# Attention's product with v for two steps at a time, in every second step

## The chip, the cores and the metric

The kernel runs on one core of one Trainium2 chip. The metric is the device time of one execution in microseconds (us); the figure for a kernel is the median over its runs. Single numbers about engines come from one profiled execution.

## The reference, cut to what matters

One encoder layer, for a prompt of 256 positions and a sample of 2048 positions, with the same weights. Positions form a grid of rows of 64. All of it is in float32.

```python
def encoder_layer(x, ...):
    h = rms_norm(x, g_pre)
    q, k, v, z_a, u_f, z_f = split(h @ w_in)
    y_a = neighbourhood_attention(q, k, v, rpb)     # 8 heads of 64; a window of 8 rows x 16 columns
    y_f = fourier_mix(u_f, w_fourier, b_fourier)
    mixed = concat([rms_norm(y_a, g_na) * silu(z_a), rms_norm(y_f, g_f) * silu(z_f)])
    return x + rms_norm(mixed @ w_out, g_post)

# neighbourhood_attention, for 16 query columns of a row against a slab of 8 rows x 32 columns
logits = q_blk @ k_slab.T * scale + bias            # outside the window: -1e30
p = softmax(logits)
out = p @ v_slab
```

## The kernel before, in words

The kernel first makes the projections (until 549 us of the profiled execution), then the Fourier branch (until about 613 us), then a loop over attention steps (613 to 865 us), and at the end the output product of the attention half. The change is in the loop over steps.

**Groups.** Attention is cut into 36 groups `G[0..35]`: four pairs of heads (`pr`), and for each pair nine groups (`i`): the prompt, and four bands of sample rows in two halves of columns each (`hc`). A group has 256 queries in two blocks `b` of 128, each with its own slab of keys, and two heads `h`.

**A step.** Step `k` (2 to 36) works on two neighbouring groups, `g = G[k]` and `f = G[k-1]`. The order in which TensorE gets its work is written by hand, and so are those of the other engines and of the DMA queue on SyncE: every engine does its instructions strictly in the order of the code. On TensorE a step is:

1. `scores(g)`: 12 products of q and k into four PSUM tiles `s`. Each is split in a high and a low part: `qh` with `kh`, `qh` with `kl`, and, last, `ql` with `kh`. They use 64 of the 128 rows of the array, one half for each head.
2. `transp(f, 0)`: the exponentials of the previous group's first block are transposed into the PSUM tiles `ptb`; ScalarE (head 0) and VectorE (head 1) copy them to a tile `pt`.
3. Six products of the Fourier half's output, `po` (`f_mm`), 128 x 512.
4. `transp(f, 1)`, and its copies.
5. Six more products of `po`.
6. `pv(f)`: the product of `pt` with v, into a PSUM tile `p` of tag `c`, of which there is one. They use 64 of the 128 columns of the array, one half for each head.

**The other engines in a step.** VectorE adds the bias and takes the maximum (`bias_max`, L1203, four times), ScalarE takes the exponential with its sum (`exps`, L1208, four times), VectorE inverts the sums and GpSimd scales (`soft`, L1215). `split_q(G[k+1])` makes the next group's `qh` on ScalarE (L1163) and `ql` on GpSimd (L1164); in ScalarE's order it stands behind the four exponentials and the copies of both transposes. `f_evac` takes `po` out of PSUM, on VectorE for even `k` (L1464), on ScalarE for odd `k` (L1461), where every second one is stored to `oD`. After `pv`, VectorE multiplies the result by the gate `za` into `y` (L1516) and ScalarE squares it (L1518 for the first pair of heads; L1522 for the others, where GpSimd adds the squares up, L1523).

**Buffers.** `pt` is a tag with two buffers of 4 KB, one for each block of a group. `v` and `za` have three buffers each. `gt` hands out tiles from a ring of 13 tiles of 4 KB; during the loop eight of them hold `wo1`, the weights of `po`, and the others take the tiles `ofs`, which `f_evac` fills.

Of the kernel before, what the change touches and what calls it, by code (L numbers as in the profile page):

```python
# [10 lines left out]
F32 = mybir.dt.float32  # L11
# [25 lines left out]
PB = 2  # L37
# [131 lines left out]
def build(tc, A, O):  # L169
# [44 lines left out]
    ps = es.enter_context(tc.tile_pool(name="ps", bufs=3, space=PSUM))  # L214
# [16 lines left out]
    def gt(shape, dtype, name):  # L231
        return gp.tile(shape, dtype, tag="g", name=name)
# [527 lines left out]
    for b in range(16):  # L760
# [13 lines left out]
        if 2 <= b < 8:  # L774
            x, y = divmod(b, 2)
# [7 lines left out]
        p = mmt(512)[:, :TP]  # L783
# [3 lines left out]
        o = st.tile([128, 256], F32, tag="f", name="f", bufs=3)  # L787
# [51 lines left out]
    for i in range(16):  # L839
        sg, pr = divmod(i, 8)  # L840
# [14 lines left out]
        o = [st.tile([128, 1024], F32, tag="f", name="f", bufs=3) for x in range(2)]  # L855
# [32 lines left out]
        for j in range(7):  # L888
# [29 lines left out]
            if sg == 0:  # L918
                x, y = divmod(7 * (pr - 1) + j, 14)
# [17 lines left out]
            for f, d in ((u_load, 0), (u_split, 4), (u_stage1, 6)):  # L937
                x = 7 * pr + j - 7 - d
# [11 lines left out]
            p = mmt(512)  # L950
# [166 lines left out]
    def group(pr, i):  # L1117
        if i == 0:
            return dict(pr=pr, R=None, ts=slice(0, TP), k0=0, nr=4, t=[(24 * b, 40) for b in range(2)])
        R, hc = divmod(i - 1, 2)  # L1120
        t0 = TP + 512 * R + 256 * hc
        return dict(pr=pr, R=R, hc=hc, ts=slice(t0, t0 + 256), k0=4 + K0[R], nr=NR[R],
                    t=[(KC0[2 * hc + b], KW[2 * hc + b]) for b in range(2)])
# [91 lines left out]
            nc.gpsimd.tensor_scalar(w, w, m[:, 4 + h:5 + h], 1.0, ALU.mult, ALU.mult)  # L1215

    G = [group(pr, i) for pr in range(4) for i in range(9)]

    sc = load_k(0)
    KK = {0: load_k(0)}  # L1220
# [5 lines left out]
    mask_p(0)  # L1226
    for g in G[:2]:
        prep(g)
# [3 lines left out]
    for n in range(2):  # L1232
        for c in range(4):
            nc.sync.dma_start(wo1[n][c].bitcast(F32),
                              woD[1, :, c, :, n * 512:n * 512 + 512].rearrange("x p d -> p x d"))
    prep(G[2])
    prep(G[3])
    for g in G[:2]:
        split_q(g)
# [3 lines left out]
    y0 = sqy.tile([128, 2, 4, 128], F32, name="y0")  # L1243
    for t, (g, x) in enumerate(zip(G, (0, 640))):
        g["w"] = []
# [69 lines left out]
    for e in range(4):  # L1315
# [26 lines left out]
        py = y_mm(e, 2)  # L1342
        scores(G[0])
        first_soft(G[0], lambda: y_out(e, 2, *py))
# [24 lines left out]
    pt = ExitStack()  # L1369
    jp = pt.enter_context(tc.tile_pool(name="jp", bufs=2))  # L1370
# [109 lines left out]
    def transp(g, b):  # L1480
        ch = g["ch"][b]
        n, z = len(ch) * 128, ch[0][1]
        o = jp.tile([128, 2, 512], F32, tag="pt", name="pt", bufs=PB)
        for h in range(2):
            for j, (c0, nk, v) in enumerate(ch):
                nc.tensor.transpose(ptb[h][:nk, j * 128:j * 128 + 128], g["w"][b][:, h, c0:c0 + nk], ident)  # L1486
            if h == 0:
                nc.scalar.copy(o[:z, h, :n], ptb[h][:z, :n])
            else:
                V.tensor_copy(o[:z, h, :n], ptb[h][:z, :n])  # L1490
        g["pt"] = g.get("pt", []) + [o]

    yt = {}

    def pv(g):
        pr, R = g["pr"], g["R"]
        p = ps.tile([128, 2, 128], F32, tag="c", name="pv", bufs=1)
        for b, ch in enumerate(g["ch"]):
            for j, (c0, nk, v) in enumerate(ch):
                for h in range(2):  # L1500
                    hs = slice(64 * h, 64 * h + 64)
                    nc.tensor.matmul(p[hs, b], g["v"][:nk, v, hs], g["pt"][b][:nk, h, j * 128:j * 128 + 128],  # L1502
                                     start=j == 0, stop=j == len(ch) - 1)
        if R is None:
            ts, hc, c = slice(0, TP), 0, 32
            za = g["za"].rearrange("p (b r c) -> p b r c", b=2, c=32)
            view = lambda a: a.rearrange("p (r b c) -> p b r c", b=2, c=32)
        else:
            ts, hc, c = slice(TP + 512 * R, TP + 512 * R + 512), g["hc"], 16
            za = g["za"].rearrange("p (r b c) -> p b r c", b=2, c=16)  # L1510
            view = lambda a: a.rearrange("p (r x b c) -> p x b r c", x=2, b=2, c=16)[:, hc]
        p4 = p.rearrange("p b (r c) -> p b r c", c=c)
        if hc == 0:
            yt[0] = jp.tile([128, 512], F32, tag="y", name="y", bufs=YB)
        y = yt[0][:, :ts.stop - ts.start]
        V.tensor_tensor(out=view(y), in0=p4, in1=za, op=ALU.mult)  # L1516
        if pr == 0:
            nc.scalar.activation(view(ysq[:, ts]), p4, AF.Square)  # L1518
        else:
            sq = jp.tile([128, 256], F32, tag="sqa", name="sqa", bufs=2)  # L1520
            s4 = sq.rearrange("p (b r c) -> p b r c", b=2, c=c)
            nc.scalar.activation(s4, p4, AF.Square)  # L1522
            nc.gpsimd.tensor_tensor(out=view(ysq[:, ts]), in0=view(ysq[:, ts]), in1=s4, op=ALU.add)  # L1523
        if R is None or hc:
            nc.sync.dma_start(yD[0, pr, :, ts], y)
# [19 lines left out]
    f_mm(1)  # L1545
    ys_split(ftiles[1])
    f_evac(1)
    pv(G[0])
    ys_load(ftiles[2])
    prep_v(G[2])  # L1550
    prep(G[4])
    for k in range(2, len(G) + 1):
        pr, i = divmod(k, 9)
        g, f = G[k] if k < len(G) else None, G[k - 1] if k else None
        if pr < 3:
            if i == 3:
                KK[pr + 1] = load_k(pr + 1)
                for x in range(2):
                    fetch_k(KK[pr + 1], pr + 1, x)
            if i == 7:  # L1560
                load_t(pr + 1, 0)
        if 0 < pr < 4 and i == 0:
            load_t(pr, 1)
        if pr < 4 and i == 3:
            load_t(pr, 2)
        if k == 9:
            nc.sync.dma_start(gpb, pbc(A["gpost"]))
        if k == 23:
            wp = pt.enter_context(tc.tile_pool(name="wp", bufs=1, side="right"))
            WO.extend(wp.tile([128, 4, D], F32R, name="w0%d" % x) for x in range(2))  # L1570
        if 24 <= k < 32:
            y = k - 24
            nc.sync.dma_start(WO[y % 2][:, y // 2].bitcast(F32), woD[0, y % 2, y // 2])
        x = k // 2 + 1
        if g:
            scores(g)
            if 2 < k < 34 and k % 2 == 0:
                ys_mul(ftiles[x])
                if x + 1 < 18:
                    ys_load(ftiles[x + 1])  # L1580
            bias_max(g, 0, 0)
            exps(g, 0, 0)
            bias_max(g, 0, 1)
            bias_max(g, 1, 0)
        if f:
            transp(f, 0)
        if g:
            exps(g, 0, 1)
            bias_max(g, 1, 1)
            exps(g, 1, 0)  # L1590
            f_mm(k, range(6))
            soft(g, 0)
            exps(g, 1, 1)
            if k in NT:
                f_norm(NT[k])
            if k in (32, 34):
                a_norm(atiles[:6] if k == 32 else atiles[6:10])
        else:
            a_mm(atiles[0], 0, range(6))
            a_norm(atiles[10:14])  # L1600
        if f:
            transp(f, 1)
        if g:
            if k + 1 < len(G):
                split_q(G[k + 1])
            soft(g, 1)
            if k == 2:
                ys_mul(ftiles[x])
                ys_load(ftiles[x + 1])
        run_later()  # L1610
        for v, x0, x1 in YSQ.get(k, []):
            nc.scalar.activation(v[:, x0:x1], v[:, x0:x1], AF.Square)
            V.tensor_tensor(out=sqs[:, x0:x1], in0=sqs[:, x0:x1], in1=v[:, x0:x1], op=ALU.add)
        if g:
            f_mm(k, range(6, 12))
        else:
            a_mm(atiles[0], 0, range(6, 12))
        if pr < 3 and i == 8:
            mask_p(pr + 1)
        if k % 2 and x < 18:  # L1620
            ys_split(ftiles[x])
        if pr < 3 and i in (5, 6, 7, 8):
            split_k(KK[pr + 1], i - 5)
        if k == 34:
            ys_split(atiles[0])
        if g:
            f_evac(k)
        if f:
            pv(f)
        if k == 12:  # L1630
            pq_.close()
        if k + 1 < len(G):
            prep_v(G[k + 1])
        if k + 3 < len(G):
            prep(G[k + 3])
        if k == 28:
            xk = [kp.tile([128, T], F32, tag=x, name="xk") for x in ("kh", "kl")]
        if 32 <= k < 36:
            x, d = k - 32, atiles[k - 32]
            d["xt"] = xk[x // 2][:, x % 2 * D:x % 2 * D + D]  # L1640
            nc.sync.dma_start(d["xt"], A["xn"][d["t"] * 128:d["t"] * 128 + 128, :])
        if k == 32:
            ys_load(atiles[0])
        if k in (34, 35):
            ys_load(atiles[k - 33])
            of_load(atiles[k - 34])
        if k == 36:
            ys_split(atiles[1])
# [113 lines left out]
```

## Time and profile before

| | |
|---|---|
| median of 3 runs | 973.16 us (972.75 to 975.66) |
| the profiled execution | 971.13 us, its span 969.3 us |
| TensorE busy | 960.3 us (99%) |
| VectorE, ScalarE, GpSimd busy | 709.3, 496.7, 430.2 us (73%, 51%, 44%) |
| granted TensorE clock | 0.997 |
| HBM | 184.37 MB read, 101.72 MB written |

PE is TensorE's product and PEld its weight load, DVE is VectorE, ACT is ScalarE, POOL is GpSimd, SP is SyncE, which issues the DMAs. The span runs from the first to the last instruction; what lies between it and the time of the execution, 1.8 us, is outside the program's instructions. A row of the timeline gives the start, the duration, the engine, the line, the operation with the tiles written and read, and how many instructions are merged in it; in square brackets stands how long the engine sat idle before, and who ended that. A product's duration includes the time in which the next one already runs, so the pace of products is read from the difference of their starts. One product of `pv` stands in the trace as two records.

### The profile page before, as it was taken

The page shows a single profiled execution, that of the slowest core. Times are in us where ns is not written, and L with a number is a line of the kernel's source. Part 1 is how long each engine was busy: PE and PEld are TensorE (multiplying, and loading weights), DVE is VectorE, ACT ScalarE, POOL GpSimd, SP SyncE. Part 2 cuts the span into 40 slices and gives each one's busy share as a digit, 9 for nine tenths or more (in the row PEclk, how much of TensorE's full clock was granted, in tenths as well). Part 3 has the DMA queues.
Part 4 walks back from the last instruction along what each step waited for, and adds up shares of the span by engine and source line. Part 5 has one row for each costly group of instructions (what it writes and reads, how often), then busy time and mean ns, then how long its engine had stood idle before and what let it go on. Part 6 is the DMA issues. An engine that isn't in the chain of part 4 may idle for free.

```text
span 969.3 us, 17001 instructions
## 1 busy us (share of the span) xinstructions
PE 960.3 (99%) x5761; PEld 805.3 (83%) x5761; DVE 709.3 (73%) x1301; ACT 496.7 (51%) x1068; POOL 430.2 (44%) x400
## 2 busy tenths in 40 slices
PE   9999999999999999999999999999999999999997
PEld 7889988888888888888888879888888888888886
DVE  6758987778986867796776446776665656659997
ACT  5836675433325533333344255677666776654443
POOL 3100003464752202766655033567677686524544
PEclk9999999999999999999999999999999999999998
DMA  9899696556849996599888897697886998979993
GB/s 327 316 378 342 239 366 241 192 203 240 324 156 379 351 409 240 208 376 342 302 304 333 303 328 298 212 297 261 260 238 222 289 328 270 286 243 343 333 345 126
DMA packets 146450, 279.89 MB, mean 289 GB/s; under 512 B 13162, under 2 KB 84284, under 8 KB 142972
## 3 DMA queue, kind: packets, MB, share of 16 engines
q1 hardware_dynamic: 145932, 278.41, 82.4%
q8 instruction: 46, 0.75, 0.3%
q10 hardware_dynamic: 432, 0.39, 0.1%
q14 instruction: 40, 0.33, 0.1%
HBM read 184.37 MB, written 101.72 MB: 295 GB/s over the span
## 4 chain that ended last, share of the span: by engine, by line
PE 97%; DVE 1%; POOL 1%; issue 0%; DMA 0%; ACT 0%; DVEq 0%; SPq 0%; POOLq 0%; ACTq 0%
PE po L1432 20%; PE mm L165 18%; PE mm L166 18%; PE mm L164 18%; PE pv L1502 5%; PE ptb L1486 5%; PE s L1181 4%; PE pab L1024 2%; PE py L164 1%; PE py L166 1%; PE py L165 1%; DMA gpre<-gpre 0%; PE ppq L1062 0%; PE pz L166 0%; PE pz L165 0%
## 5 line engine op out<-in xcount | busy, mean ns | idle before, releaser
L164 PE MATMUL mm<-xh,wa 128*128 128x512 f32 x448 | 174.4, 389 | 0.0
L165 PE MATMUL mm<-xl,wa 128*128 128x512 f32 x448 | 174.3, 389 | 0.0
L166 PE MATMUL mm<-xh,wa 128*128 128x512 f32 x448 | 174.3, 389 | 0.0
L536 POOL TENSOR_TENSOR ws<-wr 128x512 f32<-128x512 f32 x16 | 23.7, 1483 | 226.9 <-DMA wr<-wz 212.9
L1215 POOL TENSOR_SCALAR w<-w,m 128x480 f32<-128x480 f32 (+6 forms) x136 | 86.3, 647 | 44.5 <-DVE m L1212 39.3
L165 PEld LDWEIGHTS mm<-xl,wa 128*128 128x128 f32 x448 | 84.1, 188 | 17.5
L164 PEld LDWEIGHTS mm<-xh,wa 128*128 128x128 f32 x448 | 84.1, 188 | 17.5
L166 PEld LDWEIGHTS mm<-xh,wa 128*128 128x128 f32 x448 | 84.1, 188 | 17.4
L1432 PE MATMUL po<-wo,yh 128*128 128x512 f32 x272 | 90.5, 413 | 0.0
L551 DVE TENSOR_TENSOR wa<-wr,wa 128x512 fp32r<-128x512 f32 x60 | 68.6, 1152 | 27.9 <-ACT wa L550 27.7
L1208 ACT ACTIVATE w<-w,m 128x480 f32<-128x480 f32 (+6 forms) x136 | 79.3, 586 | 15.2 <-DVE m L1203 15.2
L1432 PE MATMUL po<-w,yh 128*128 128x512 f32 x280 | 86.7, 391 | 0.0
L1203 DVE CUSTOM_DVE_ANT_1 w<-s,tb 128x360 f32<-128x360 f32 (+5 forms) x124 | 62.5, 541 | 8.1 <-PE s L1181 7.3
L589 POOL TENSOR_TENSOR mt<-mt,rmask 128x880 f32<-128x880 f32 (+2 forms) x24 | 51.1, 2141 | 33.9 <-DVE mt L585 27.4
L165 PE MATMUL mm<-vl,xh 128*128 128x512 f32 x168 | 65.5, 390 | 0.2 <-DVE vl L482 0.2
L164 PE MATMUL mm<-vh,xh 128*128 128x512 f32 x168 | 65.4, 389 | 0.0
L166 PE MATMUL mm<-vh,xl 128*128 128x512 f32 x168 | 65.4, 389 | 0.0
L877 DVE TENSOR_TENSOR f<-u,mm 128x512 f32<-128x512 f32 x64 | 43.5, 680 | 28.1 <-PE mm L166 23.5
L1432 PEld LDWEIGHTS po<-w,yh 128*128 128x128 f32 x280 | 52.3, 188 | 10.8 <-issue 0.2
L1486 PE MATMUL ptb<-ident,w 128*120 128x128 f32 (+5 forms) x428 | 59.6, 277 | 0.1
L550 ACT CAST wa<-wr 128x512 fp32r<-128x512 f32 x60 | 36.4, 617 | 45.1 <-PE mm L166 18.8
L1490 DVE COPY pt<-ptb 120x384 f32<-120x384 f32 (+6 forms) x72 | 41.0, 570 | 24.5 <-PE ptb L1486 24.0
(253 smaller groups left out, 2402.9 us busy)
## 6 DMA issues: line engine op xcount, KB each, us to landing
wr<-wz SPq DMA_DIRECT2D x48, 512.0 KB
vl<-sD SPq DMA_DIRECT2D x20, 512.0 KB
xm<-xm SPq DMA_DIRECT2D x9, 1024.0 KB
oD<-ofs SPq DMA_DIRECT2D x18, 512.0 KB
of<-oD SPq DMA_DIRECT2D x18, 512.0 KB
yr<-yD SPq DMA_DIRECT2D x34, 256.0 KB
zD<-f SPq DMA_DIRECT2D x16, 512.0 KB
woD<-wo SPq DMA_DIRECT2D x16, 512.0 KB
```

Source lines behind the costliest of these rows:

```text
L164: nc.tensor.matmul(out, lh, rh, start=first, stop=False)
L165: nc.tensor.matmul(out, lh, rl, start=False, stop=False)
L166: nc.tensor.matmul(out, ll, rh, start=False, stop=last)
L551: nc.vector.tensor_tensor(out=o[:, 1], in0=src, in1=o[:, 0].bitcast(F32), op=ALU.subtract)
L589: nc.gpsimd.tensor_tensor(out=o, in0=i, in1=rmask[:, m0:m0 + n].unsqueeze(2).to_broadcast([128, n, 80]), op=ALU.add)
L877: nc.vector.tensor_tensor(out=dst(f, b), in0=src(uu[u]), in1=src(p), op=op)
L1203: nc.vector.tensor_tensor_reduce(out=rows(g["w"][b][:, h, :n], w), in0=rows(g["s"][2 * b + h][:, :n], w), in1=tv, scale=1.0, scalar=3.0e38 ...
L1208: nc.scalar.activation(w, w, AF.Exp, bias=m[:, h:h + 1], scale=-1.0, accum_out=m[:, 2 + h:3 + h])
L1215: nc.gpsimd.tensor_scalar(w, w, m[:, 4 + h:5 + h], 1.0, ALU.mult, ALU.mult)
L1432: nc.tensor.matmul(p, (d["l"] if x == 2 else d["h"])[:, c], w(n, int(x == 1), c), start=j == 0, stop=j == 11)
L1486: nc.tensor.transpose(ptb[h][:nk, j * 128:j * 128 + 128], g["w"][b][:, h, c0:c0 + nk], ident)
L1502: nc.tensor.matmul(p[hs, b], g["v"][:nk, v, hs], g["pt"][b][:nk, h, j * 128:j * 128 + 128], start=j == 0, stop=j == len(ch) - 1)
```

## The change

`pv` no longer runs in every step. In every even step `k` it takes two groups, `G[k-2]` and `G[k-1]`: first all products of both, into one PSUM tile of twice the size (2 KB instead of 1 KB for each partition), then the multiplication by the gate and the squares of the first group, then those of the second. The call ahead of the loop goes. Since the transposed exponentials of the even group now wait for the next step, they are kept in a tile of the ring (`gt`); those of the odd group stay in the tag `pt`.

```diff
     G = [group(pr, i) for pr in range(4) for i in range(9)]
+    for k, g in enumerate(G):
+        g["k"] = k
...
     def transp(g, b):
         ch = g["ch"][b]
         n, z = len(ch) * 128, ch[0][1]
-        o = jp.tile([128, 2, 512], F32, tag="pt", name="pt", bufs=PB)
+        if g["k"] % 2:
+            o = jp.tile([128, 2, 512], F32, tag="pt", name="pt", bufs=PB)
+        else:
+            o = gt([128, 2, 512], F32, "pt")
...
-    def pv(g):
-        pr, R = g["pr"], g["R"]
-        p = ps.tile([128, 2, 128], F32, tag="c", name="pv", bufs=1)
+    def pv(k):
+        p = ps.tile([128, 2, 2, 128], F32, tag="c", name="pv", bufs=1)
+        for x in range(2):
+            pv_mm(G[k + x], p[:, x])
+        for x in range(2):
+            pv_out(G[k + x], p[:, x])
+
+    def pv_mm(g, p):
         for b, ch in enumerate(g["ch"]):
             for j, (c0, nk, v) in enumerate(ch):
                 for h in range(2):
                     hs = slice(64 * h, 64 * h + 64)
                     nc.tensor.matmul(p[hs, b], g["v"][:nk, v, hs], g["pt"][b][:nk, h, j * 128:j * 128 + 128],
                                      start=j == 0, stop=j == len(ch) - 1)
+
+    def pv_out(g, p):
+        pr, R = g["pr"], g["R"]
         if R is None:
...
-    pv(G[0])
     ys_load(ftiles[2])
...
-        if f:
-            pv(f)
+        if k % 2 == 0:
+            pv(k - 2)
```

TensorE before, at the end of step 13 and the start of step 14 (`po` the Fourier product, `pv` the attention's, `s` the scores):

```order
L1432 MATMUL po<-wo_5180,yh 128x512 x2
L1432 MATMUL po<-wo_5180,yl 128x512
L1502 MATMUL pv<-pt,v 64x128 x14
L1181 MATMUL s<-kh,qh 128x360 x2
L1181 MATMUL s<-kl,qh 128x360 x2
L1181 MATMUL s<-kh,ql 128x360 x2
```

The 14 products with v stand between `po` and the scores. TensorE now, at the same place:

```order
L1434 MATMUL po<-wo_5180,yh 128x512 x2
L1434 MATMUL po<-wo_5180,yl 128x512
L1181 MATMUL s<-kh,qh 128x360 x2
L1181 MATMUL s<-kl,qh 128x360 x2
L1181 MATMUL s<-kh,ql 128x360 x2
```

The scores of step 14 follow `po` of step 13 directly. TensorE now, at the end of step 14 and the start of step 15:

```order
L1434 MATMUL po<-wo_5176,yh 128x512 x2
L1434 MATMUL po<-wo_5176,yl 128x512
L1513 MATMUL pv<-pt,v 64x128 x28
L1181 MATMUL s<-kh,qh 128x480 x2
L1181 MATMUL s<-kl,qh 128x480 x2
```

The products of step 13 have moved here, ahead of those that stood here before. VectorE before, from the end of step 12 to the first score tiles of step 13, with the engines that each instruction waits for (`ofs` is `f_evac`, `y` the gate, L1203 is `bias_max`, of which the program holds two rows each):

```order
L1464 TENSOR_SCALAR ofs<-po,invf 128x512 [waits PE_49]
L1516 TENSOR_TENSOR y<-pv,za 128x2x8x16 [waits DMAHW3_49,PE_49]
L1203 ISA w,m<-s,tb 128x480 [waits PE_49]
L1203 ISA m 128x1
L1203 ISA w,m<-s,tb 128x480 [waits PE_49]
```

One `y` stands ahead of the first `bias_max`. VectorE now, at the same place:

```order
L1466 TENSOR_SCALAR ofs<-po,invf 128x512 [waits PE_49]
L1530 TENSOR_TENSOR y<-pv,za 128x2x8x16 [waits DMAHW1_49,DMAHW0_49,PE_49]
L1530 TENSOR_TENSOR y<-pv,za 128x2x8x16 [waits DMAHW3_49,Activation_49]
L1203 ISA w,m<-s,tb 128x480 [waits DVE_49,PE_49]
L1203 ISA m 128x1
```

Two stand there now. The first waits for TensorE, with the semaphore value of the last of the 28 products; the second waits for ScalarE, with the value of the square of the first group.

## The prediction

> **What bounds the kernel now.** I read the page first, then the chain of work that ended last, then the stretch of the loop by windows, then its waits, and last the timeline of single steps.
>
> ```profile
> span 969.3 us, 17001 instructions
> PE 960.3 (99%) x5761; PEld 805.3 (83%) x5761; DVE 709.3 (73%) x1301; ACT 496.7 (51%) x1068; POOL 430.2 (44%) x400
> PE 97%; DVE 1%; POOL 1%; issue 0%; DMA 0%; ACT 0%; DVEq 0%; SPq 0%; POOLq 0%; ACTq 0%
> ```
>
> TensorE is busy for 99% of the span and makes up 97% of the chain. So a gain is TensorE time taken away, and whatever makes TensorE wait is a loss at its full price. For the loop the window says the same:
>
> ```profile
> core 0: us, PE busy (x) PEld busy (x) DVE busy (x) ACT busy (x) POOL busy (x), PEclk, DMA share, GB/s
> 613.00:872.00 259.00, 258.88 (x2261) 213.01 (x2260) 166.38 (x523) 172.56 (x491) 170.64 (x227) 1.00 0.87 266
> ```
>
> TensorE idles 0.12 us in 259. Over 36 steps of some 7.2 us the others average 4.6 to 4.8 us a step, which looks like room. But the change makes the steps uneven, and then what counts is the latency from one step's scores to the next step's work, not the mean. Here is step 13 (odd) and the start of step 14; VectorE, ScalarE and GpSimd all belong to this chain.
>
> ```profile
> 694.50 0.49 PE L1181 MATMUL s<-kh,qh 64*128 64x480 f32 x2
> 694.62 0.43 DVE L1516 TENSOR_TENSOR y<-pv,za 128x256 f32<-128x256 f32 x1 [0.25 <-PE pv L1502]
> 695.14 0.39 ACT L1522 ACTIVATE sqa<-pv 128x256 f32<-128x256 f32 x1 [2.91 <-DVE y L1516]
> 695.47 0.66 DVE L1203 CUSTOM_DVE_ANT_1 w<-s,tb 128x480 f32<-128x480 f32 x1 [0.42 <-PE s L1181]
> 696.17 0.70 ACT L1208 ACTIVATE w<-w,m 128x480 f32<-128x480 f32 x1 [0.65 <-DVE m L1203]
> ...
> 699.54 0.41 ACT L1163 CAST qh<-ql 128x256 fp32r<-128x256 f32 x1
> 699.99 0.40 PE L1432 MATMUL po<-wo,yl 128*128 128x512 f32 x1
> 700.03 0.73 POOL L1164 TENSOR_TENSOR ql<-ql,qh 128x256 fp32r<-128x256 f32 x1 [0.33 <-ACT qh L1163]
> 700.31 1.75 PE L1502 MATMUL pv<-pt,v 120*64 120x128 f32 x28
> 701.99 0.44 PE L1181 MATMUL s<-kh,qh 64*128 64x360 f32 x2
> 702.43 0.33 PE L1181 MATMUL s<-kh,ql 64*128 64x360 f32 x2
> ```
>
> ```profile
> 696.17:699.95 3.78, 3.78 (x25) 3.29 (x23) 2.81 (x10) 3.78 (x12) 1.49 (x3) 1.00 1.01 314
> ```
>
> The first maximum (695.47) lets ScalarE begin its exponentials at 696.17. From there to the end of `qh` at 699.95 ScalarE is busy for 3.78 of 3.78 us, without a gap. GpSimd follows with `ql`, ready at 700.76, and step 14's scores use it from their third pair on, at 702.43. The slack is 1.67 us, and the visit of `pv` at 700.31 is what makes it.
>
> **What the change takes away.** In an odd step the scores start where `pv` started, at 700.31 instead of 701.99: 1.68 us earlier. (The last `po` product starts at 699.99; to the next instruction of another shape of the array it was 0.32 us, and directly to scores I expect the same, by the rows below.) In the even step the second group's 14 products are added at their own pace:
>
> ```profile
> 649.63 1.64 PE L1502 MATMUL pv<-pt,v 120*64 120x128 f32 x26
> 642.15 1.75 PE L1502 MATMUL pv<-pt,v 120*64 120x128 f32 x28
> ```
>
> Two records more take 0.11 us, so 28 take 1.54. The saving of a visit is 1.68 - 1.54 = 0.14 to 0.15 us: the cost of changing into the shape of `pv` (0.32 instead of 0.23 us after `po`, and a slower first product). The change out of it stays, as one into scores. That full-array products are followed by scores at the same price I take from the one place where it happens now:
>
> ```profile
> 602.76 0.34 PE L165 MATMUL py<-abl,pqh 128*128 128x384 f32 x1
> 602.93 0.34 PE L166 MATMUL py<-abh,pql 128*128 128x384 f32 x1
> 603.20 0.39 PE L1181 MATMUL s<-kh,qh 64*128 64x264 f32 x1
> 603.43 0.28 PE L1181 MATMUL s<-kl,qh 64*128 64x264 f32 x1
> 603.54 0.28 PE L1181 MATMUL s<-kh,ql 64*128 64x264 f32 x1
> ```
>
> The pace is 0.17, the step into scores 0.27 (0.10 more), and the first pair of scores takes 0.23 instead of 0.11. 18 visits go (the call ahead of the loop and odd steps 3 to 35): 18 x 0.15 = 2.7 us. The ends: 0.05 a visit if scores after `po` cost 0.10 more than here (0.9 us), 0.35 if they cost nothing (6.3 us).
>
> **What it adds: lateness at the start of odd steps.** After an even step there are now two `y` and two squares. The first `y` waits for the last of 28 products, as it waited for the last of its own before, so it starts at the same distance from the scores (694.62). The square of the first group waits for it, the second `y` waits for that square, and only then comes the first `bias_max`. By the rows of step 13: `y` to 695.05, square 695.14 to 695.53, second `y` about 695.56 to 695.98, and `bias_max` at about 695.93 (on VectorE one starts some 0.05 before the last one's record ends) instead of 695.47. That is 0.46 us late. The cover that existed was 0.42 us of idle VectorE; it is used up by half of this chain. Since ScalarE has no gap from the exponentials to `qh`, `ql` comes 0.46 us later as well.
>
> That the second `y` must wait for a square that only reads the same tile is also what the Trainium skill says, in "PSUM — Partial Sum Buffer", section "PSUM bank collisions raise a hardware error": two engines must not be in one bank and quadrant of partitions at a time, reads included, so software must keep them apart. In this trace the square is always behind `y` (the wait below agrees); no run here shows a collision. If reads could overlap, the second `y` would end at 695.48, `bias_max` would not be late at all, and the time would be that of the second rival.
>
> ```profile
> ACT sqa L1522 <- DVE y L1516: 48.4, 26, 3.2
> ```
>
> **The sum at the odd-to-even border.** In step 14 the scores come 1.68 us earlier and `ql` 0.46 us later, against a slack of 1.67, of which some 0.05 go to the hand-over (those between engines in these rows take 0.02 to 0.09): TensorE waits 1.68 + 0.46 - 1.67 + 0.05 = 0.52 us. I did the same for all 16 borders from 3/4 to 33/34; the first and the last:
>
> ```profile
> 621.43 0.43 PE L1181 MATMUL s<-kh,qh 64*128 64x360 f32 x2
> 622.21 0.53 DVE L1203 CUSTOM_DVE_ANT_1 w<-s,tb 128x360 f32<-128x360 f32 x1 [0.15 <-PE s L1181]
> 626.59 0.74 POOL L1164 TENSOR_TENSOR ql<-ql,qh 128x256 fp32r<-128x256 f32 x1 [0.47 <-ACT qh L1163]
> 627.00 1.53 PE L1502 MATMUL pv<-pt,v 118*64 118x128 f32 x24
> 628.46 0.49 PE L1181 MATMUL s<-kh,qh 64*128 64x480 f32 x2
> 629.01 0.38 PE L1181 MATMUL s<-kh,ql 64*128 64x480 f32 x2
> ...
> 837.37 0.66 DVE L1203 CUSTOM_DVE_ANT_1 w<-s,tb 128x480 f32<-128x480 f32 x1 [0.42 <-PE s L1181]
> 841.93 0.73 POOL L1164 TENSOR_TENSOR ql<-ql,qh 128x256 fp32r<-128x256 f32 x1 [0.33 <-ACT qh L1163]
> 842.21 1.75 PE L1502 MATMUL pv<-pt,v 120*64 120x128 f32 x28
> 843.88 0.41 PE L1181 MATMUL s<-kh,qh 64*128 64x288 f32 x2
> 844.25 0.30 PE L1181 MATMUL s<-kh,ql 64*128 64x288 f32 x2
> ```
>
> First: visit 1.46 (628.46 - 627.00), `bias_max` at 621.43 + 1.34 = 622.77 instead of 622.21, so 0.56 late, slack 629.01 - 627.33 = 1.68: wait 0.39. Last: 1.67 + 0.46 - 1.59 + 0.05 = 0.59. The sixteen in order are 0.38, 0.31, 0.36, 0.14, 0.39, 0.53, 0.61, 0.65, 0.66, 0.47, 0.50, 0.41, 0.23, 0.45, 0.54, 0.59: together 7.2 us. The lateness in them is 0.2 to 0.8 us; steps whose first score tile is narrow have more, since their `bias_max` starts earlier now. Lower end: with no lateness five borders still wait, 0.65 us in all. Upper end: with 0.1 us more at every border (each hand-over between engines a little dearer), 8.8.
>
> Other consumers behind the missing visit (the scaled exponentials for `transp`, the split `y` tile, the evacuated `po`) have, with the wait above, 0 to 1.5 us left each; they add nothing but some 0.1 us. `transp(f, 1)` in odd steps needs the copies of `transp(f, 0)`, which the lateness also shifts; they keep 0.07 us or more. Border 35/36 has no scores; the transposes come 1.5 us earlier there, and their inputs are just ready. At no other border is anything late: before odd steps the longer `pv` gives 1.5 us more.
>
> **The ring and the queues.** The even group's `pt` goes to the ring, of which five tiles turn over, three per two steps. Its copy in an odd step may have to wait until the store of `ofs` from two steps ago has left the tile:
>
> ```profile
> 686.18 0.41 SPq L1462 DMA_DIRECT2D oD<-ofs  x1
> 699.08 0.57 ACT L1488 COPY pt<-ptb 120x512 f32<-120x512 f32 x1
> ```
>
> 12.9 us lie between, and the visit moved into the even step between adds to that; I cost it at nothing. On SyncE the load of v in even steps now waits for the first group's products, and `za` and later loads queue behind it; what they bring is used two steps later, so nothing. GpSimd adds both squares up at the start of odd steps, where it is idle until `soft`.
>
> **Sum.** 971.13 (the profiled execution) - 2.7 + 7.2 = 975.6. The median of the runs is 2.0 above that execution, so the forecast is 977.6 us, +4.5.
>
> **The rivals.**
> - *Not slower: the lateness does not reach `ql`.* Then TensorE waits 0.65 us and the time is 973.16 - 2.7 + 0.65 = 971.1. It decides from a total wait under 2.7 us, 0.17 a border. For it: VectorE averages only 4.6 us a step. Against it: ScalarE's 3.78 of 3.78, and the second `y` behind the square. The Trainium skill's rule that a change of tiling mode drains TensorE ("TensorEngine Tiling (Array Packing)", section "Key Properties") counts for this side: alone, it gives the -2.7, 970.5.
> - *Slower still: the ring.* If a store of `ofs` is not out when the copy wants its tile, ScalarE stops, and with it `qh` and the scores. The transfers' share in the loop is 0.87, which speaks for it, the 12.9 us against. A stop of 0.3 us at each of 16 borders gives 4.8 more: 982.4.
> - *The bigger saving:* scores after `po` without a drain: 973.16 - 6.3 + 7.2 = 974.1; the rows at 602.93 and 603.20 speak against it.
>
> **How the numbers follow.** My forecast 0.74; the ring or a dearer hand-over 0.07; the lateness absorbed 0.14; the bigger saving 0.05. The range, 973.8 to 981.5, goes from the bigger saving to 8.8 us of waits with some trouble in the ring; it leaves out the absorbed case and the worst of the ring. A measurement here can tell 0.3% (2.9 us) from no change. Faster than 970.2 is only the tail of the absorbed case, 0.04. Between there and 976.1 lie the rest of it, the bigger saving and the low end of my own, 0.17. Slower: 0.79.
>
> **What would show it.** In the profile after: TensorE's idle time in the loop rises from 0.1 to some 7 us, all of it in even steps at the scores' third pair (L1181, `ql`), put down to GpSimd's L1164; in odd steps the first maximum starts about 1.3 us after the scores instead of mostly 0.7 to 1.0, behind two `y` with a square between; the scores follow `po` in 0.32 us with no `pv` between. If TensorE's idle stays under 2.7 us, the step on lateness is wrong; if waits appear at the copies of `pt` for a DMA, the ring is.

## The result, and the profile after

The changed kernel takes 980.76 us (median of 6 runs, 979.89 to 983.37), the kernel before took 972.76 us beside it (6 runs): 8.0 us more, a ratio of 1.0083 with a 95% interval of 1.0068 to 1.0099. The forecast was 977.6 us, in a range from 973.8 to 981.5. The profiled execution took 983.37 us, the longest of the six. These are lines of its page, the window of the loop (the counterpart of 613 to 872 before), and TensorE's own waits in that window:

```profile
span 981.6 us, 16958 instructions
PE 966.1 (98%) x5761; PEld 806.9 (82%) x5761; DVE 709.6 (72%) x1301; ACT 495.4 (50%) x1068; POOL 430.2 (44%) x400
PE 90%; DMA 3%; DVE 2%; ACT 1%; POOL 1%; issue 1%; DVEq 0%; SPq 0%; POOLq 0%; ACTq 0%
```

```profile
615.50:883.90 268.40, 262.69 (x2261) 213.45 (x2259) 164.06 (x523) 170.66 (x487) 170.01 (x227) 0.99 0.84 255
```

```profile
PE s L1181 <- POOL ql L1164: 2.0, 8, 0.4
PE ptb L1491 <- POOL kl L1096: 1.4, 1, 1.4
PE s L1181 <- ACT qh L1163: 1.3, 1, 1.3
PE ptb L1491 <- ACT pt L1493: 0.4, 1, 0.4
```

TensorE carried 97% of the chain before; now it carries 90%, and the other engines appear in it. Not all of that is loss in the loop: from 319.6 to 350.3 us, 3% of the span, the chain runs through DMAs and other engines in the projections, while TensorE was busy, because one product there then waited 0.6 us. Four kinds of waits over 0.15 us stand in the loop where there was none. (A line of waits gives the sum in us, how many, and the longest.) The idle times are too small, though: a product's record covers time in which the next one would already run. So I measure TensorE's loss from the starts of its products, step by step, against the trace of before. From the first `po` to the last `pv` product the loop takes 9.4 us longer in this execution (606.63 to 865.13 before, 609.12 to 877.03 now); another 2.5 us lie ahead of the loop, in code that the change does not touch. (1.4 us of them are there by 10 us, where the first products run at half the pace, as the last section shows, and 0.8 come at 348 to 350 us.) The lines that answer to those of step 13 and 14 before:

```profile
698.38 0.49 PE L1181 MATMUL s<-kh,qh 64*128 64x480 f32 x2
698.50 0.42 DVE L1530 TENSOR_TENSOR y<-pv,za 128x256 f32<-128x256 f32 x1 [2.04 <-PE pv L1513]
698.95 0.38 ACT L1536 ACTIVATE sqa<-pv 128x256 f32<-128x256 f32 x1 [3.10 <-DVE y L1530]
699.37 0.42 DVE L1530 TENSOR_TENSOR y<-pv,za 128x256 f32<-128x256 f32 x1 [0.45 <-ACT sqa L1536]
699.71 0.65 DVE L1203 CUSTOM_DVE_ANT_1 w<-s,tb 128x480 f32<-128x480 f32 x1
...
703.78 0.40 ACT L1163 CAST qh<-ql 128x256 fp32r<-128x256 f32 x1
704.23 0.43 PE L1181 MATMUL s<-kh,qh 64*128 64x360 f32 x2
704.26 0.73 POOL L1164 TENSOR_TENSOR ql<-ql,qh 128x256 fp32r<-128x256 f32 x1 [0.33 <-PE po L1434]
704.50 0.33 PE L1181 MATMUL s<-kl,qh 64*128 64x360 f32 x2
705.04 0.43 PE L1181 MATMUL s<-kh,ql 64*128 64x360 f32 x2 [0.22 <-POOL ql L1164]
```

It is the chain of the prediction. The second `y` starts 0.04 us after the first square ends, the first maximum comes 1.33 us after the scores instead of 0.97, and `ql` is there so late that the third pair of scores starts 0.81 us after the first instead of 0.44. The row shows 0.22 us of idle time; step 14's scores take 0.48 us longer to the next transposes, of which 0.37 lie ahead of the third pair and 0.11 behind it (1.03 us from there to the transposes instead of 0.92).

Two places the prediction did not have. At the border of steps 17 and 18:

```profile
736.50 1.56 POOL L1113 TENSOR_TENSOR tb<-cm,tb 128x640 f32<-128x640 f32 x1
738.02 1.40 POOL L1096 TENSOR_TENSOR kl<-kl,kh 128x576 fp32r<-128x576 f32 x1
738.09 0.33 DVE L1203 CUSTOM_DVE_ANT_0 w<-s,tb 128x160 f32<-128x160 f32 x1 [2.41 <-POOL tb L1113]
738.89 0.46 ACT L1493 COPY pt<-ptb 128x384 f32<-128x384 f32 x1
739.49 0.83 PE L1491 MATMUL ptb<-ident,w 128*96 128x128 f32 x6 [1.43 <-POOL kl L1096]
```

The first maximum of step 18 needs the masked table `tb`, which GpSimd makes behind `ql` and `soft`. VectorE stands for 2.41 us, its copies and those of ScalarE behind it, and the second transposes wait for the copies. And at the border of steps 29 and 30 the load of `ql` itself comes late: SyncE has stood for 6.16 us at a load of v and issues it only behind that. First the same load of v in the kernel before, then the changed one:

```profile
802.45 2.10 SPq L1154 DMA_DIRECT2D v<-vD  x1
```

```profile
809.40 6.16 SPq L1154 DMA_DIRECT2D v<-vD  x1
815.66 0.62 SPq L1159 DMA_DIRECT2D za<-zD  x1
816.32 0.43 SPq L1135 DMA_DIRECT2D ql<-qD  x1
820.54 0.40 ACT L1163 CAST qh<-ql 128x256 fp32r<-128x256 f32 x1 [1.27 <-DMA ql<-qD]
821.00 0.43 PE L1181 MATMUL s<-kh,qh 64*128 64x360 f32 x2 [1.29 <-ACT qh L1163]
```

A smaller third place is step 4, where VectorE is late. Two additions of squares, the first of which waited 0.82 us for ScalarE's square, and the split of `yl` stand ahead of the first maximum, which starts 2.69 us after the scores (629.42) instead of 1.13:

```profile
629.72 1.48 DVE L1626 TENSOR_TENSOR sqs<-sqs,Y 128x256 f32<-128x256 f32 x2 [0.82 <-ACT Y L1625]
631.12 1.06 DVE L1425 TENSOR_TENSOR yl<-yr,yh 128x512 fp32r<-128x512 f32 x1
632.11 0.64 DVE L1203 CUSTOM_DVE_ANT_1 w<-s,tb 128x480 f32<-128x480 f32 x1
```

### The profile page after: what moved, and what is told of

Same layout as the page of the kernel before. It is cut to its first block, busy times and chain, and to the rows that moved or that the text cites. A ratio compares the mean times of both kernels' runs of the same rounds, so it can differ in the third digit from the quotient of the medians.

```text
span 981.6 us, 16958 instructions
## 1 busy us (share of the span) xinstructions
PE 966.1 (98%) x5761; PEld 806.9 (82%) x5761; DVE 709.6 (72%) x1301; ACT 495.4 (50%) x1068; POOL 430.2 (44%) x400
## 4 chain that ended last, share of the span: by engine, by line
PE 90%; DMA 3%; DVE 2%; ACT 1%; POOL 1%; issue 1%; DVEq 0%; SPq 0%; POOLq 0%; ACTq 0%
PE po L1434 18%; PE mm L165 17%; PE mm L164 17%; PE mm L166 17%; PE pv L1513 5%; PE ptb L1491 5%; PE s L1181 3%; DMA wr<-wo 2%; PE pab L1024 2%; PE py L164 1%; PE py L166 1%; PE py L165 1%; POOL ql L1164 1%; ACT w L1208 1%; DVE wo L713 0%
## 5 line engine op out<-in xcount | busy, mean ns | idle before, releaser
L551 DVE TENSOR_TENSOR wa<-wr,wa 128x512 fp32r<-128x512 f32 x60 | 72.4, 1214 | 26.7 <-ACT wa L550 26.6
L1203 DVE CUSTOM_DVE_ANT_1 w<-s,tb 128x360 f32<-128x360 f32 (+5 forms) x124 | 62.3, 539 | 1.1 <-PE s L1181 0.9
L1491 PEld LDWEIGHTS ptb<-ident,w 128*120 128x120 f32 (+5 forms) x428 | 47.0, 136 | 14.8 <-issue 9.1
```

The source lines that it names most:

```text
L551: nc.vector.tensor_tensor(out=o[:, 1], in0=src, in1=o[:, 0].bitcast(F32), op=ALU.subtract)
L1203: nc.vector.tensor_tensor_reduce(out=rows(g["w"][b][:, h, :n], w), in0=rows(g["s"][2 * b + h][:, :n], w), in1=tv, scale=1.0, scalar=3.0e38 ...
```

## The experiments

Each was timed in turns with the kernel before, on one chip in each of three rounds; the ratio is to that kernel in the same round. "Loop" is the difference of the loop to that of the trace of before, by starts of products. I call the edits by what they do.

**The account of the loop**, worked out from the starts of the products in each trace. "third pair" is the time from the first score product to the first transposes in even steps, "first pair" the odd-to-even borders against the saving of a visit that nothing disturbs, "copies" the time between the two transposes (step 30 left out, in odd steps the scores' waits too), "step 30" all that is late from border 29/30 to step 31, the saving is that of the last row's kernel, where almost nothing waits.

| kernel | median, us | ratio (95%) | third pair | first pair | copies | step 30 | saving | loop |
|---|---|---|---|---|---|---|---|---|
| changed | 980.76 | 1.0083 (1.0068 to 1.0099) | 6.3 | 0.9 | 2.1 | 2.9 | -2.8 | +9.4 |
| changed, again | 980.92 | 1.0074 (1.0054 to 1.0094) | 6.0 | 0.8 | 2.1 | 1.0 | -2.8 | +7.1 |
| ring alone | 972.66 | 1.0001 (0.9992 to 1.0009) | 0 | 0 | 0 | 0 | 0 | +0.03 |
| both y first | 978.06 | 1.0053 (1.0037 to 1.0069) | 2.1 | 0 | 1.9 | 1.4 | -2.8 | +2.5 |
| y and squares late | 978.06 | 1.0050 (1.0038 to 1.0062) | 3.6 | 0 | 2.6 | 0 | -2.8 | +3.8 |
| qh and ql early | 979.92 | 1.0071 (1.0057 to 1.0085) | 2.2 | 0.1 | 4.1 | 3.7 | -2.8 | +7.3 |
| load of ql ahead | 980.66 | 1.0073 (1.0057 to 1.0090) | 6.3 | 0.9 | 2.1 | 0.9 | -2.8 | +7.5 |
| mask early | 978.84 | 1.0051 (1.0032 to 1.0070) | 6.3 | 0.8 | 0.7 | 1.2 | -2.8 | +6.2 |
| all moves | 973.30 | 0.9999 (0.9988 to 1.0010) | 1.0 | 0 | 1.0 | 0.3 | -2.8 | -0.3 |
| all moves, mended | 971.59 | 0.9982 (0.9969 to 0.9995) | 0 | 0 | 0 | 0 | -2.8 | -2.0 |
| v with two buffers | 974.32 | 1.0020 (1.0000 to 1.0041) | 0 | 0 | 0.2 | 0 | 0 | +0.2 |

What a row lacks to its sum is a tenth or two of rounding, and 0.2 to 0.8 us in the last step, told below where it matters.

**The changed kernel once more**

> The changed kernel once more, unedited, for a second trace. What belongs to the kernel must come back at the same steps with the same size: the waits for ql in even steps (6.7 us in all, of which some 0.35 at step 30), 0.55 at step 4, 1.3 at step 18. What depends on how long single transfers take may differ: 2.4 us around step 30, where the load of ql came late, and 2.5 us ahead of the loop. So a loop between 869 and 873 us shorter or longer by the late load alone, and 980.8 us within 1 in the median. If the late places move to other steps, the explanation by mask and queue is wrong.

Measured 980.92 us. The 16 waits come back within 0.02 us each but for steps 30 and 32, step 4 with 0.56 and step 18 with 1.32. Only step 30 differs, 1.0 us instead of 2.9. So the first two kinds belong to the kernel, and the third is there in both, with a size that depends on the transfers. Ahead of the loop this execution lost 0.2 us, not 2.5.

**The ring alone**

```diff
-        o = jp.tile([128, 2, 512], F32, tag="pt", name="pt", bufs=PB)
+        if g["k"] % 2:
+            o = jp.tile([128, 2, 512], F32, tag="pt", name="pt", bufs=PB)
+        else:
+            o = gt([128, 2, 512], F32, "pt")
```

> The kernel before, with only the ring part: the even group's pt comes from the ring, pv runs in every step as before. If the ring costs nothing: 973 us, within 0.5. If copies wait for the store of ofs to leave its tile, as the rival of the prediction has it, 0.3 us at 16 steps: 977.8.

972.66 us beside 973.24, and no step of the loop differs by more than 0.03 us from before. The ring costs nothing here. In the changed kernel, where a group's tile is held a step longer, no copy into `pt` waits for a DMA either; that rival is out.

**Both y first**

```diff
         for x in range(2):
             pv_out(G[k + x], p[:, x])
+        for x in range(2):
+            pv_sq(G[k + x])
```

`pv_out` keeps `y` and its store; `pv_sq` is the square and GpSimd's sum.

> Both y first, then the two squares; nothing else differs from the changed kernel. Lateness theory (6.7 us of TensorE's waits in even steps come from the first bias_max of the odd step, which starts late behind y, square, y): the second y no longer waits for a square, so bias_max starts where it did before the change (about 0.85 us after the scores); the first exponential now waits for the second square, about 0.2 us later than before the change. Each wait shrinks by about 0.26 us, the sum from 6.7 to about 2.4: 980.8 - 4.3 = 976.5 us. The other late places (steps 4, 18 and 30, 4.3 us in all) stay. Rival, the ring or the queue of loads makes the whole loss: the time stays at 980.8, and the waits for ql stay at 6 to 7 us.

978.06 us, 1.6 above the 976.5 expected. The waits at the third pair fall from 6.3 to 2.1 us (2.4 expected), those at the first pair vanish. Step 13 of it:

```profile
695.11 0.49 PE L1181 MATMUL s<-kh,qh 64*128 64x480 f32 x2
695.23 0.76 DVE L1532 TENSOR_TENSOR y<-pv,za 128x256 f32<-128x256 f32 x2 [2.04 <-PE pv L1515]
696.08 0.66 ACT L1545 ACTIVATE sqa<-pv 128x256 f32<-128x256 f32 x2 [3.18 <-PE s L1181]
696.08 0.66 DVE L1203 CUSTOM_DVE_ANT_1 w<-s,tb 128x480 f32<-128x480 f32 x1
```

The two `y` run without a square between, and the maximum is back at 0.97 us after the scores. So the lateness is that of the square between them, and it is what most of the waits for `ql` were made of: this one exchange of order takes 4.2 us from the third pair and 0.9 from the first. Steps 4 and 18 stay as they were. The median fell by 2.8 us, less than the trace, which is that of its fastest run (974.82 of 974.82 to 980.86).

**y and squares late**

```diff
             bias_max(g, 1, 1)
+            if k % 2:
+                for o in outs:
+                    pv_out(*o)
+                za_load(g)
...
+        if g and k % 2:
+            for o in outs:
+                pv_sq(o[0])
         if g:
             f_evac(k)
```

> The gate products y and the squares leave the start of the odd step: y stands behind the fourth bias_max, the squares behind split_q (their sums on GpSimd behind soft), and the load of za for the odd group comes behind y. Lateness theory: the first bias_max starts as soon as its scores are there (0.35 us after them instead of 1.3), ql comes some 0.9 us earlier than in the changed kernel, and the waits for ql fall from 6.7 us to under 1. The store of y also leaves its place ahead of the load of v in SyncE's queue, so the late load of ql at step 30 (2.4 us) may go with it; the wait for the mask in step 18 (1.3) stays. 980.8 - 6.2 = 974.6 us, 972.2 if step 30 goes as well. Rival, the ring or the price of longer visits: no change, 980.8.

978.06 us, a miss: 3.5 more than the 974.6 expected, and 5.9 more than the 972.2 for the case that step 30 comes clean, which it does. The maximum comes at once (0.97 us after the scores, which is the time that the 480-column scores themselves take, so my 0.35 was wrong), yet the third pair still waits for 3.6 us in all. (The copies cost 2.6 us as well, 1.3 of them still in step 18.) Here is why, from step 13:

```profile
698.83 0.66 DVE L1208 CUSTOM_DVE_ANT_1 w<-s,tb 128x480 f32<-128x480 f32 x1 [2.36 <-PE s L1186]
...
701.36 0.75 DVE L1540 TENSOR_TENSOR y<-pv,za 128x256 f32<-128x256 f32 x2
702.02 0.15 DVE L1217 RECIPROCAL m<-m 128x2 f32<-128x2 f32 x1
702.35 1.32 POOL L1220 TENSOR_SCALAR w<-w,m 128x480 f32<-128x480 f32 x2 [5.90 <-PE ptb L1496]
702.90 0.41 ACT L1168 CAST qh<-ql 128x256 fp32r<-128x256 f32 x1
703.63 0.73 POOL L1169 TENSOR_TENSOR ql<-ql,qh 128x256 fp32r<-128x256 f32 x1
704.41 0.43 PE L1186 MATMUL s<-kh,ql 64*128 64x360 f32 x2 [0.16 <-POOL ql L1169]
```

`qh` is ready at 703.31, but `ql` starts at 703.63: GpSimd is still at `soft`, which waited for the reciprocal, which now waits for the two `y`. The lateness had moved from ScalarE's chain to GpSimd's. Step 30 is clean here (0 us): the load of v holds SyncE for 2.75 us instead of 6.16, and the load of `ql` for step 30 is issued 6.1 us ahead of that step's scores (811.46 to 817.58) instead of 4.7 (816.32 to 821.00). The store of `y` no longer stands ahead of the loads of v and `ql`, but the load of `za` and the squares moved as well; which of the moves does it, this run does not tell.

**qh and ql early**

```diff
             soft(g, 0)
+            if k % 2 and k + 1 < len(G):
+                split_q(G[k + 1])
             exps(g, 1, 1)
```

> In odd steps alone split_q stands ahead of the fourth exponential and the copies of the second transposes, so ql no longer comes at the end of ScalarE's chain; the lateness of bias_max itself stays. If the lateness costs time through the chain on ScalarE to ql and nowhere else, the waits for ql fall from 6.7 us to under 0.7 with bias_max still 1.3 us behind the scores: about 974.5 us. If lateness also costs through the copies and the scaled exponentials, the waits turn up at the transposes of the even steps and the time stays within 1.5 us of 980.8. At step 30, where the load of ql itself is late, ScalarE now stops earlier in the step, so that place costs the same or up to 1 us more by both.

979.92 us: the second case. The waits at the third pair fall from 6.3 to 2.2 us, so most of the path to `ql` was indeed ScalarE's chain; under 0.7 was expected if it had been all of it. But what stands behind on ScalarE is later, and half of the cost turns up again at the copies and at the `po` tile (4.1 us instead of 2.1). At step 30 it costs 3.7 us, since ScalarE now stands for the late load (2.64 us) ahead of its last exponential.

**The load of ql ahead**

```diff
+        if k + 3 < len(G):
+            prep(G[k + 3])
         if k % 2 == 0:
             pv(k - 2)
```

> The changed kernel with the load of ql for three steps on issued ahead of the store of y and the loads of v and za, instead of behind them; nothing else. Theory that SyncE's queue, which the later v loads hold up, makes ql late at step 30: the stop there (1.3 us at the scores, 0.4 at ql, 1.1 behind the transposes) goes, and the slowest runs with it: 978.5 us if it happens in most runs, 980.0 if only in some. Rival, the transfers themselves are late (their share is above 0.8 in the loop) whatever the order of the queue: no change, 980.8.

980.66 us, no change. The stop at the scores is gone, but at the end of the same step the products with v now wait:

```profile
818.62 3.62 SPq L1154 DMA_DIRECT2D v<-vD  x1
822.30 0.83 SPq L1152 DMA_DIRECT2D v<-vD  x1
827.79 0.88 PE L1513 MATMUL pv<-pt,v 88*64 88x128 f32 x12 [0.41 <-DMA v<-vD]
```

The load of v whose last part is issued at 822.30 serves the products of the same step. So at this place the queue is late as a whole, and this change of order within it only chose who pays.

**Two buffers for v in the kernel before**

```diff
-        g["v"] = jl.tile([128, 7, 128], F32, tag="v", name="v", bufs=VB)
+        g["v"] = jl.tile([128, 7, 128], F32, tag="v", name="v", bufs=2)
```

> The kernel before, with two buffers for v instead of three and nothing else: the load of v for the next step must wait for the products of the step it stands in, as it now does in the even steps of the changed kernel; no products are moved. If the lost lead of these loads is what makes loads late around step 30, TensorE waits there for v or ql here too, 0.5 to 3 us: 973.1 + 0.5 to 3. If the transfers are late there for another reason (the squares, stores of y in pairs, chance), the trace shows no wait there and the time stays at 973.1.

974.32 us beside 973.01, with runs from 972.46 to 981.47. The loss of lead alone may cost something (the interval begins at 1.0000), and two of the 12 runs took over 981 us, but its trace (of a run of 972.83) shows no wait at step 30 and only 0.2 us at step 33. That step 30's lateness comes from the lost lead is therefore not shown. What is shown is that it is gone or small (0 to 0.3 us) in the three versions in which `y` and its store stand later, together with the load of `za` and the squares.

**The mask early**

```diff
             f_mm(k, range(6))
+            if pr < 3 and i == 8:
+                mask_p(pr + 1)
             soft(g, 0)
```

> The changed kernel with mask_p on GpSimd ahead of the first soft of its step instead of behind the second one; nothing else. Theory that the 1.3 us at step 18 are the first bias_max waiting for the mask, which stands in GpSimd behind ql and soft, both late now: the gap of 1.43 us at the transposes of step 18 goes, everything else stays: 980.8 - 1.3 = 979.5 us. Rival, another thing is late at the same place: the gap stays and the time too.

978.84 us, some 2 us less than the changed kernel's two medians; by the loop's account 1.3 at step 18 and 0.3 gained beyond. The gap of 1.43 us is gone: the maximum starts without waiting, and so do the transposes, though `kl`, which the row of the changed kernel named as the releaser, still runs at the same place:

```profile
735.08 0.31 DVE L1203 CUSTOM_DVE_ANT_0 w<-s,tb 128x160 f32<-128x160 f32 x1
735.99 1.44 POOL L1096 TENSOR_TENSOR kl<-kl,kh 128x576 fp32r<-128x576 f32 x1
737.37 0.82 PE L1491 MATMUL ptb<-ident,w 128*96 128x128 f32 x6
```

Step 18 is even 0.27 us shorter than before the change: there the mask was already the last, by a little.

**All moves together, and mended**

```diff
             f_mm(k, range(6))
+            if pr < 3 and i == 8:
+                mask_p(pr + 1)
             soft(g, 0)
+            if k % 2:
+                for o in outs:
+                    pv_out(*o)
+                za_load(g)
...
-    YSQ = {2: ..., 3: [(Y, 256, 512), (Y2, 1024, 1664)], 4: ...
+    YSQ = {2: ..., 3: [(Y, 256, 512)], 8: [(Y2, 1024, 1664)], 4: ...
```

The late squares and the early load of `ql` are as above; `y` stands one place later than there, behind the first `soft`.

> All of it together: y behind the first soft of the odd step (so that VectorE's reciprocal and GpSimd's ql come before it), the squares behind split_q, mask_p early, the load of ql early, and one of the additions of squares on VectorE moved from step 3 to step 8. If the four named causes are all there is, the waits for ql fall to about 0.7 us, the places at steps 4, 18 and 30 are gone, and what is left is the saving of the missing visits, 1.9 to 2.7 us: 973.2 - 2.2 + 0.7 = 971.7 us, below the kernel before. If something else costs as well (longer visits, the ring, more transfers at once), it stays above 973.2.

973.30 us, as fast as before but no faster. So 7.5 us of the changed kernel's time are gone; 1.6 us were left over the expectation, in places most of which the moves made: the squares ahead of `f_evac` hold up the `po` tile in steps 6 and 8 (0.3 and 0.4 us), the early mask holds up `ql` in step 27 (0.5), the third pair keeps 1.0. The place at step 4, 0.6 to 1.2 us in all versions of the changed kernel so far, is gone with the addition that left step 3. The mended version (the mask of even steps goes back to its old place):

```diff
-            if pr < 3 and i == 8:
+            if pr < 3 and i == 8 and k % 2:
                 mask_p(pr + 1)
...
+        if k % 2 and k + 1 < len(G):
+            split_q(G[k + 1])
         if f:
             transp(f, 1)
...
         if g:
             f_evac(k)
+        if g and k % 2:
+            for o in outs:
+                pv_sq(o[0])
```

> The version with all moves, with three more: the squares stand behind the evacuation of po instead of ahead of it (in steps 5 and 7 they made it late, and TensorE waited 0.3 and 0.4 us for the tile), the mask is early in step 17 alone (in step 26 it held ql up, 0.47 us), and split_q of odd steps stands ahead of the copies of the second transposes (the waits left for ql are 1.0 us in all). If these are what is left between the saving and the kernel before, the loop becomes 1.8 us shorter than in the version with all moves: 973.3 - 1.8 = 971.5 us, 1.6 below the kernel before. Rival: each move makes something else late, as the first ones did, and it stays at 973 or above.

971.59 us (12 runs) beside 973.01 (23 runs): faster than the kernel before by 1.4 us (by the interval of the ratio 0.5 to 3.0), and than the changed one by 9.2. Its span and, of the waits in the loop, those of TensorE:

```profile
span 970.2 us, 16933 instructions
```

```profile
PE pna L1483 <- POOL ysq L1554: 0.5, 1, 0.5
PE ptb L1496 <- POOL kl L1096: 0.2, 1, 0.2
```

No even step waits for `ql`. Two places are left: the norm in step 36, for which GpSimd's last sums are late (0.8 us by starts), and step 6 (0.3). Some of the 1.4 us, the 0.3 of step 18, would probably be open to the kernel before too; that was not tried. The saving itself, 2.8 us, lies at the borders where the visits of `pv` are missing.

## Why the prediction was right in direction and short in size

- **The saving of 2.7 us: right.** Where nothing waits (all moves, mended), the visit ahead of the loop and the odd steps give 0.96 + 26.27 us back, and the even steps and step 36 take 23.21 + 1.2: 2.8 us, 0.16 a visit.
- **The waits of 7.2 us: right.** Measured 6.0 to 6.3 us at the third pair and 0.8 to 0.9 at the first, 6.8 to 7.2 together, and in the first trace at each of the 15 borders without a late load within 0.15 us of the forecast's figure. That some of it would be spent waiting for `qh`, ahead of the first pair, I had not said. Their cause is shown by the exchange of `y` and square, most of their path by `qh` and `ql` moved forward. Luck has a part in so close a sum: 1.6 us of it are lost behind the third pair, 0.1 in each even step (in step 4 the next pair follows the third after 0.32 us instead of 0.22). The forecast had no such term; what lies ahead of the two pairs, as it reckoned, comes to 5.6 us (in step 13 the first maximum comes 1.33 us after the scores, its rows gave 1.43).
- **"They add nothing but some 0.1 us" (the other consumers behind the missing visit): wrong, 2.1 us.** They are waits of second transposes for the copies, in the even steps 4 (0.6) and 18 (1.3) above all; in the odd steps, of which "they keep 0.07 us or more" was said, the copies cost only 0.1 us in all. I shifted only the lateness of the first maximum by its usual 0.2 to 0.8 us. In step 18 the maximum has another thing to wait for, the mask, and once the scores come 1.4 us earlier that wait is 2.41 us instead of 1.26. In the waits of before it stands in a row that I had not followed:

```profile
DVE w L1203 <- POOL tb L1113: 2.6, 3, 1.3
```

  In step 4 it is VectorE's backlog of additions and splits. Both are places where an engine that averages 64 to 66% of the loop is full for most of a step: GpSimd is busy for 6.13 of the 6.40 us from 733.0, VectorE for 4.28 of the 4.30 from 629.7.
- **"What they bring is used two steps later, so nothing" (SyncE's queue): wrong, 0.9 to 3.7 us** in the six traces with the store of `y` ahead of the loads, at one place (step 30). There one issue of a load of v holds SyncE for 4.24 to 6.16 us in these six traces, and for 2.10 to 4.14 in the others; in five of the six the load of `ql` stands behind it, in the sixth a later load of v. What makes the issue longer is open: the same line took 5.57 us at 677.05 in the changed kernel and cost TensorE nothing.
- **The ring at nothing: right**, within 0.03 us. With it the other rivals are out: the lateness was not absorbed (6.8 us and more of waits against 0.65), and the saving is 0.16 us a visit, not 0.35.
- **What the trace would show:** the idle time of some 7 us, "all of it in even steps at the scores' third pair", was misjudged. By records the loop idles 5.7 us, and only 2.3 of them lie there (2.0 in the eight waits that the line shows), since idle time between records is not the time lost.

So the sum 2.7 and 7.2 stands; the terms put at 0.1 and nothing measured 2.1 and 1.0 to 2.9. That is 3 to 5 us, and the median was 3.5 us above the forecast's step of 4.5. It lies in the range all the same, 0.7 us below its top. That top was set for dearer hand-overs and trouble in the ring, which did not come; that the range was wide enough for two waits of another kind is luck. Of the 2.5 us ahead of the loop nothing is explained by the change: the other traces have 0.2 to 4.2 there, and those of kernels with `pv` in every step 0 to 1.1. Whether that is chance with so few traces stays open.

## What to carry to other kernels

Work that is gathered into every second step makes two kinds of steps. The saving is read from the borders, but each engine's backlog must be followed through both kinds, including the steps that carry something extra (a mask, a table, a norm), and an average share of busy time says nothing about them. Before giving up such a change, look at the order on the other engines: here most of the loss was one of order, and the best of the orders tried turned a loss of 8 us into a gain of 1.4.

## What the runs showed of the hardware that I had not expected

- TensorE's idle time by records is less than half of what a wait costs here: 0.22 us idle against 0.48 lost in step 14, 2.3 against 6.3 us for the kind. The pair ahead of such a wait has a record of 0.33 us (704.50), where the next pair would have started 0.22 us later (step 14 before: 0.44 us for two pairs).
- The releaser that the profile names can be a bystander: `kl` was named for the 1.43 us of step 18, and moving the mask alone removed them.
- Some executions begin at half the pace. These are the first products of the changed kernel and of its second trace, in the same code (start, duration; the steady pace is 0.23 us):

```profile
8.12 0.63 PE L164 MATMUL mm<-wc,xh 128*128 128x512 f32 x1
8.54 0.63 PE L165 MATMUL mm<-wc,xh 128*128 128x512 f32 x1
```

```profile
8.20 0.39 PE L164 MATMUL mm<-wc,xh 128*128 128x512 f32 x1
8.43 0.39 PE L165 MATMUL mm<-wc,xh 128*128 128x512 f32 x1
```

  The stretch lasts for 5 to 8 products and costs 1.1 to 1.5 us, in four of the twelve traces. In the version with all moves its granted clock is 0.50; in the changed kernel the profile gives 1.00 for the same pace, so a lower clock stands beside the slow pace in that one trace only:

```profile
8.00:10.00 2.00, 2.00 (x6) 1.63 (x5) 1.97 (x5) 1.98 (x5) 0.00 (x0) 0.50 0.76 214
```
